# A two-block network on one core: the recurrences of layer 0 taken apart, with GEMMs put between their pieces

## Chip, core and metric

The kernel runs on one core of one Trainium2 chip. The metric is the device time of one execution in microseconds (us); most executions of a kernel agree within 0.3%. The engines are TensorE (PE; its weight loads are PEld), VectorE (DVE), ScalarE (ACT), GpSimd (POOL) and SyncE (SP, which issues most DMAs). They run side by side and wait for one another by semaphores.

## What is computed

The program is a two-layer network for 512 tokens of width 1024, followed by a second network of one layer. Each of the two layers has a mixer and a mixture of 16 experts. Only the mixer of layer 0 is touched. It projects its input once and feeds two branches: a bidirectional gated recurrence over 512 channels with a gate of its own, and a Hyena branch of 512 channels, two long convolutions done by FFT matrices. `_adaln` gives the shifts, scales and gates ("modulation") of both layers from one vector, a product with a 1024 x 6144 matrix per layer.

```python
def _adaln(cvec, w_mod, b_mod, n_chunks):
    m = jax.nn.silu(cvec) @ w_mod[:, :n_chunks * D_MODEL] + b_mod[:n_chunks * D_MODEL]
    return [m[:, None, j * D_MODEL:(j + 1) * D_MODEL] for j in range(n_chunks)]

def _rglru(xa_raw, p, h0):
    xa = _dwconv1d(xa_raw, p['conv_a_w'], p['conv_a_b'])
    ...
    r = gate(p['lru_wr'], p['lru_br'])          # sigmoid of a product per head
    i = gate(p['lru_wi'], p['lru_bi'])
    log_a = -LRU_C * r * jax.nn.softplus(-p['lru_lam'].astype(f32))[:, None, None, :]
    a = jnp.exp(log_a)
    u = jnp.sqrt(-jnp.expm1(2.0 * log_a)) * i * xa.astype(f32)[None]
    ...
    a_cum, h = lax.associative_scan(_lin_combine, (a, u), axis=2)
    ...

def _even_mixer(h, p, h0):
    proj = h @ p['w_in']
    gate = proj[..., :RNN_WIDTH]
    xa_raw = proj[..., RNN_WIDTH:2 * RNN_WIDTH]
    hy = proj[..., 2 * RNN_WIDTH:]
    hs, h_last = _rglru(xa_raw, p, h0)
    y_a = jax.nn.gelu(gate) * (hs[0] + jnp.flip(hs[1], axis=1)).astype(h.dtype)
    u = _dwconv1d(hy, p['conv_b_w'], p['conv_b_b'])
    v, *gates = jnp.split(u, HYENA_ORDER + 1, axis=-1)
    kf = _hyena_filters_fft(h.shape[1], p)
    z = v
    for o in range(HYENA_ORDER):
        z = gates[o] * _fftconv(z, kf[:, o], p['filt_bias'][o])
    return jnp.concatenate([y_a, z], axis=-1) @ p['w_out'], h_last
```

The recurrence's initial state comes from a context of 256 tokens, so a scan runs over 256 and then 512 tokens, in both directions.

## The kernel before, around the change

The activations lie with channels on the partitions: a channel tile `ct` is 128 channels by 512 tokens. Layer 0 (`layer0`) works the Hyena branch in two halves of 256 channels, and the recurrence in two pairs of channel tiles. Its order in the program:

- the filter spectra `K` of the first Hyena half, the first modulation block, the normalization;
- in one scope: `hyena_in(0, "mm")`, the first half's input products; `hyena(.., 0, ..)`, its convolutions, with the modulation unit (0, 1) fed between its steps; the products that enter the recurrence, `xax` and, for the context, `xac`;
- in the next scope: `lru` for channel tiles 0 and 1, then `lru` for 2 and 3, with the modulation units (0, 2) and (1, 0) fed into them; then the second half's `filters`; then its input products, `hyena_in(1, "ac")`;
- in a third scope: `hyena(.., 1, ..)`; then the four GEMMs of the recurrence's gate with GELU, multiplied into `cat`; then `part`, which splits each finished channel tile in a high and a low fp32r half, and `project`, the output projection, which ends in the routing of the experts.

A GEMM (`gemm_block`, `gemm3`, L351) takes 24 matmuls of 128x512 in fp32r: eight steps of the contraction, three products of halves. Its weights come as a block of 1 MB (`cblock`, `rload`, L318), good for two GEMMs; each GEMM's half of it is split by an ACT copy (`wsplit`, L340, tile `wsh`) and a subtraction (`sub`, L334, tile `wsl`), of which every third goes to POOL and the others to DVE. After a GEMM, `conv_tap` evicts it (ACT, L629) and adds the other taps on DVE (L635).

`lru` has two parts: for each channel tile, matmuls (L653) and tanh (L655) of the gates, tanh and exp (L660, L661) and a DVE product (L663); then for both tiles one square root (L668), two DVE products (L670, L671), eight scans (L674, L675) and a POOL sum (L677). Its tiles `lr` and `li` have two buffers, one for each channel tile of a pair; `lt`, of both tiles, has one.

`filters` first makes ten sums and differences in the tile `filtF` (matmuls L593, DVE L594 to L616, some on POOL), then 18 matmuls (L623) for `K`.

A modulation unit (l, i) is eight blocks of 1 MB; `mod_mm` (L448) issues four matmuls a block, the profile records each fp32 matmul twice. `mod_units` is a generator: `mod_feed(n)` runs n blocks of it. The blocks have the tile `mblk` with two buffers.

What sets the order. Each engine and each DMA queue executes its instructions in a fixed order, made when the program is built: a scheduler takes the instructions in program order, but lets a later one that is ready go ahead while an earlier one waits. A tile is given out by a pool: `ring` has four buffers of 1 MB for all streamed weights; PSUM has eight banks under three tags, `mm` (four), `tr` (two) and `ac` (two). A pool that is opened after another was closed may lie on its memory, and its tiles then wait for the earlier ones to be done with. `project` writes its end (`TAIL`) in an order by hand, and the experts' loads (`expert_load`) follow on SP's queue, behind four reloads of `x` (L811) into the memory that `z` and `xac` had.

Of the kernel before, what the change touches and what calls it, by code (L numbers as in the profile page):

```python
# [10 lines left out]
F32 = mybir.dt.float32  # L11
# [7 lines left out]
P = 128  # L19
# [250 lines left out]
class Builder:  # L270
# [214 lines left out]
    def mod_units(self, mp, tag, units, bufs):  # L485

        nc, a = self.nc, self.a
        for l, i in units:
            p = self.mm(tag)
            for k in range(KD):  # L490
                w = mp.tile([P, 2048], F32, tag="mblk", name=self.nm("mblk"), bufs=bufs)
                nc.sync.dma_start(out=w, in_=a["w_mod"][l, k * P:(k + 1) * P, 2048 * i:2048 * (i + 1)])
                self.mod_mm(p, w, k)
                if k < KD - 1:
                    yield
            if i:

                r = slice(0, 64) if i == 1 else slice(64, 128)
                nc.vector.tensor_tensor(self.modr[r, l], p[r], self.modr[r, l], op=ALU.add)
            q = self.mod_turn(mp, p)  # L500
            for h, n, b in {0: ((0, 0, "bsh1"), (1, 1, "bsc1")), 1: ((1, 2, "bsh2"),), 2: ((0, 3, "bsc2"),)}[i]:
                self.mod_put(self.modc[:, l, n], q, h, 0, self.col(b, 8 * l, 8))
            yield
# [134 lines left out]
    def lru(self, kp, wp, cts, xac, xax, hb, s2, s4, cat):  # L638

        nc, a = self.nc, self.a  # L640
        st = []
        tt = wp.tile([P, 2, 2, 768], F32, tag="lt", name=self.nm("lt"))
        for ct in cts:
            lw = kp.tile([P, 512], F32, tag="gt", name=self.nm("lruw")).rearrange("p (g c) -> p g c", g=4) if ct % 2 else \
                wp.tile([P, 4, P], F32, tag="lruw", name=self.nm("lruw"))
            nc.gpsimd.dma_start(out=lw, in_=a["lruw"][:, ct * 512:(ct + 1) * 512].rearrange("p (g c) -> p g c", g=4))
            r, i = (wp.tile([P, 2, 768], F32, tag=n, name=self.nm(n), bufs=2) for n in ("lr", "li"))
            t = tt[:, len(st)]
            for xa, o, n in ((xac[:, ct], 0, 256), (xax[:, ct], 256, 512)):
                for d in range(2):  # L650
                    for g, dst in ((0, r), (1, i)):
                        p = self.mm()
                        nc.tensor.matmul(p[:, :n], lw[:, 2 * d + g], xa, start=True, stop=True)  # L653

                        nc.scalar.activation(out=dst[:, d, o:o + n], in_=p[:, :n], func=AF.Tanh, scale=0.5,  # L655
                                             bias=hb[:, 8 * g + 4 * d + ct:8 * g + 4 * d + ct + 1])

            for d in range(2):
                c = slice(4 * d + ct, 4 * d + ct + 1)
                nc.scalar.activation(out=t[:, d], in_=r[:, d], func=AF.Tanh, scale=s2[:, c], bias=s2[:, c])  # L660
                nc.scalar.activation(out=r[:, d], in_=r[:, d], func=AF.Exp, scale=s4[:, c], bias=s4[:, c])  # L661
            for xa, o, n in ((xac[:, ct], 0, 256), (xax[:, ct], 256, 512)):
                nc.vector.scalar_tensor_tensor(i[:, :, o:o + n], i[:, :, o:o + n], 1.0, xa[:, None, :].to_broadcast([P, 2, n]),  # L663
                                               op0=ALU.add, op1=ALU.mult)
            st.append((ct, r, i, t))
            self.mod_feed(4)
        f = lambda x: x.rearrange("p d n -> p (d n)")
        nc.scalar.activation(out=tt, in_=tt, func=AF.Sqrt)  # L668
        for ct, r, i, t in st:
            nc.vector.scalar_tensor_tensor(f(t), f(r), 1.0, f(t), op0=ALU.add, op1=ALU.mult)  # L670
            nc.vector.scalar_tensor_tensor(f(t), f(t), 0.5, f(i), op0=ALU.mult, op1=ALU.mult)  # L671
            for o, n, ini in ((0, 256, (0.0, 0.0)), (256, 512, (i[:, 0, 255:256], i[:, 1, 0:1]))):
                s = slice(o, o + n)
                nc.vector.tensor_tensor_scan(i[:, 0, s], r[:, 0, s], t[:, 0, s], ini[0], op0=ALU.mult, op1=ALU.add)  # L674
                nc.vector.tensor_tensor_scan(i[:, 1, s][:, ::-1], r[:, 1, s][:, ::-1], t[:, 1, s][:, ::-1], ini[1],  # L675
                                             op0=ALU.mult, op1=ALU.add)
            nc.gpsimd.tensor_tensor(cat[:, ct], i[:, 0, 256:768], i[:, 1, 256:768], op=ALU.add)  # L677

    def layer0(self):
        nc, a, tc = self.nc, self.a, self.tc  # L680
        es = ExitStack()
        kp = es.enter_context(tc.tile_pool(name="A", bufs=1, reuse_waits="tile"))
        cat = kp.tile([P, KD, 512], F32, name="cat0")
        self.fc0 = kp.tile([P, 2, P], F32, name="fc0")
        K = kp.tile([P, 9, 2, 256], F32, name="K")
        self.h2 = kp.tile([65, 512], F32, name="h2")
        self.nrow0 = kp.tile([P, 3], F32, name="nrow0")
        lam = kp.tile([P, 2, 8], F32, name="lamc")
        hb = kp.tile([P, 16], F32, name="lruhb")
        x = self.x  # L690
        w = ExitStack()
        wp = w.enter_context(tc.tile_pool(name="A1", bufs=1, reuse_waits="tile"))
# [8 lines left out]
        rt, fcs = self.filter_blocks(0, fpool)  # L701

        wn = ExitStack()
        wq = wn.enter_context(tc.tile_pool(name="A2n", bufs=1, reuse_waits="tile"))
# [39 lines left out]
        z = xf[:, 0:3072].rearrange("p (q c n) -> p q c n", q=3, c=2)  # L744
        xac = xf[:, 3072:4096].rearrange("p (c n) -> p c n", c=4)
        xax = cat[:, 0:4]

        def hyena_in(hf, tag):
            for q in range(3):
                wt = self.cblock(wi, (1024 + 512 * q + 256 * hf, 256))  # L750
                for c in range(2):
                    ct = 4 * q + 2 * hf + c
                    p = self.gemm_block(kp, wt, c, h, tag)
                    self.conv_tap(z[:, q, c], p, 512, "cbw", self.col("cbb", ct), ct, 12, 1, 3)
                yield


        w = ExitStack()
        wp = w.enter_context(tc.tile_pool(name="A4", bufs=1, reuse_waits="tile"))
# [18 lines left out]

        w = ExitStack()
        wp = w.enter_context(tc.tile_pool(name="A2", bufs=1, reuse_waits="tile"))  # L780
        mw = ExitStack()
        self.mod_begin(mw.enter_context(tc.tile_pool(name="Amb", bufs=1, reuse_waits="tile")), "tr", ((0, 2), (1, 0)))
        self.lru(kp, wp, (0, 1), xac, xax, hb, lam[:, 0], lam[:, 1], cat)
        self.lru(kp, wp, (2, 3), xac, xax, hb, lam[:, 0], lam[:, 1], cat)
        self.mod_end()
        mw.close()
        wq = w.enter_context(tc.tile_pool(name="A3", bufs=1, reuse_waits="tile"))
        rt, fcs = self.filter_blocks(1)
        list(self.filters(wq, rt, fcs, K, "ac"))
        for _ in hyena_in(1, "ac"):  # L790
            pass
        w.close()

        w = ExitStack()
        wp = w.enter_context(tc.tile_pool(name="A4b", bufs=1, reuse_waits="tile"))
        self.hyena(wp, 1, K, z)
        for q in range(2):
            wt = self.cblock(wi, (256 * q, 256))
            for c in range(2):
                ct = 2 * q + c  # L800
                p = self.gemm_block(kp, wt, c, h, "ac")
                gt = kp.tile([P, 512], F32, tag="gt", name=self.nm("gt"))
                last = nc.scalar.activation(out=gt, in_=p, func=AF.Gelu_apprx_tanh)
                nc.gpsimd.tensor_tensor(cat[:, ct], cat[:, ct], gt, op=ALU.mult)
        parts = self.hparts("cp")
        for ct in range(6):
            self.part(parts, ct, cat[:, ct])
# [7 lines left out]
        w = ExitStack()  # L815
        wp = w.enter_context(tc.tile_pool(name="A5", bufs=1, side="right", reuse_waits="tile"))
        gate = self.bcast_gate(wp, 0, 0)
# [1654 lines left out]
```

## Time and profile before

| | |
|---|---|
| time, median of 3 runs | 2370.78 us (2370.53 to 2378.63) |
| the profiled execution's own time | 2370.2 us |
| its span, first to last instruction | 2368.1 us |
| mean granted clock of TensorE | 0.963 |
| busy share of the span: PE, DVE, ACT, POOL | 92%, 43%, 26%, 15% |
| read from HBM, mean rate | 545.51 MB, 232 GB/s |

A busy time is the union of an engine's instructions. The matmuls' ends are modelled, so that a busy TensorE is not one at its peak; the granted clock is given as a share of full speed. The layers' mixtures of experts and the second network take most of the span; the stage of the change is some 185 us long.

### The profile page before, as it was taken

How to read it: one execution, taken by the hardware profiler on the slowest of the kernel's cores; microseconds unless marked ns; L12 is line 12 of the kernel's file. 1: busy time of each engine (PE TensorE's matmuls, PEld its weight loads, DVE VectorE, ACT ScalarE, POOL GpSimd, SP SyncE). 2: the span in 40 equal slices, each digit the busy share in tenths (PEclk: the TensorE clock that was granted, in tenths of full speed). 3: DMA queues.
4: the chain of work that ended last, by engine and by line, in shares of the span. 5: the costliest groups of instructions: out<-in, count | busy, mean ns of one | idle time of the engine just before them, and what ended most of it. 6: DMA issues, size and time to landing. Idle time of an engine off the chain costs nothing.

```text
span 2368.1 us, 29818 instructions
## 1 busy us (share of the span) xinstructions
PE 2183.7 (92%) x11928; PEld 1319.5 (56%) x11928; DVE 1025.3 (43%) x2051; ACT 614.8 (26%) x1149; POOL 361.0 (15%) x390
## 2 busy tenths in 40 slices
PE   7997899999998987999899998987999889999998
PEld 2772487554342424667554433334766667777776
DVE  5645563622121214883522221215665666535642
ACT  3336123210000004333200000005433334333442
POOL 2221113000000002012000000002233431232232
PEclk9998799989999999999889999998999999999999
DMA  8537215679999997744789999996211220141131
GB/s 323 190 106 266 107 61 209 244 321 419 418 419 418 419 419 274 249 160 160 301 324 420 420 420 420 420 418 207 71 37 46 79 63 28 37 151 45 45 112 71
DMA packets 190196, 551.64 MB, mean 233 GB/s; under 512 B 12625, under 2 KB 69849, under 8 KB 182762
## 3 DMA queue, kind: packets, MB, share of 16 engines
q1 hardware_dynamic: 186282, 533.47, 58.4%
q0 software_dynamic: 2768, 11.71, 1.5%
q10 hardware_dynamic: 1008, 4.56, 0.5%
q8 instruction: 94, 1.54, 0.3%
q14 instruction: 44, 0.36, 0.0%
HBM read 545.51 MB, written 4.19 MB: 232 GB/s over the span
## 4 chain that ended last, share of the span: by engine, by line
PE 60%; DMA 13%; DVE 5%; POOL 3%; ACT 2%; issue 1%; POOLq 0%; DVEq 0%; ACTq 0%; SPq 0%
PE mm L1166 14%; DMA ring<-in_exp_w_dram 12%; PE ac L1166 6%; PE ac L1553 4%; PE mm L904 4%; PE ac L1554 4%; PE ac L1555 4%; PE mm L351 4%; PE mm L1662 2%; PE tr L1127 2%; PE ac L351 2%; PE ac L1127 2%; PE ac L1275 1%; PE tr L1275 1%; PE tr L1710 1%
## 5 line engine op out<-in xcount | busy, mean ns | idle before, releaser
L1166 PE MATMUL mm<-ring,xsT 128*64 128x512 f32 x2048 | 472.2, 596 | 38.1 <-DMA ring<-in_exp_w_dram 38.1
L1166 PEld LDWEIGHTS mm<-ring,xsT 128*64 128x64 f32 x2048 | 149.8, 137 | 328.1 <-issue 250.0
L1166 PE MATMUL ac<-ring,em 128*64 128x512 f32 x896 | 203.9, 601 | 13.2 <-DMA ring<-in_exp_w_dram 12.3
L1553 PE MATMUL ac<-hC,sth 128*128 128x512 f32 x504 | 211.5, 420 | 1.7 <-ACT msg L2249 1.7
L1554 PE MATMUL ac<-hC,sth 128*128 128x512 f32 x504 | 206.5, 410 | 0.0
L1555 PE MATMUL ac<-hC,stl 128*128 128x512 f32 x504 | 204.4, 406 | 0.2 <-DVE stl L334 0.2
L1166 PEld LDWEIGHTS ac<-ring,em 128*64 128x64 f32 x896 | 64.7, 138 | 142.1 <-issue 111.3
L1529 ACT ACTIVATE sth<-ring 128x512 fp32r<-128x512 f32 x126 | 79.2, 630 | 145.9 <-PE ac L1554 127.7
L1255 DVE TENSOR_TENSOR em<-em,mm 128x512 f32<-128x512 f32 x32 | 21.8, 688 | 218.9 <-PE mm L1166 216.9
L1553 PEld LDWEIGHTS ac<-hC,sth 128*128 128x128 f32 x504 | 96.6, 192 | 25.9 <-ACT msg L2249 4.0
L1267 DVE SCALAR_TENSOR_TENSOR ac<-ac,gts,gate 128x512 f32<-128x512 f32 x28 | 21.2, 759 | 204.5 <-PE ac L1166 204.5
L1555 PEld LDWEIGHTS ac<-hC,stl 128*128 128x128 f32 x504 | 96.2, 191 | 20.9 <-DVE stl L334 0.7
L1554 PEld LDWEIGHTS ac<-hC,sth 128*128 128x128 f32 x504 | 96.4, 191 | 20.1 <-issue 2.1
L1276 DVE TENSOR_TENSOR x<-ac,x 128x512 f32<-128x512 f32 x64 | 41.6, 686 | 140.8 <-PE ac L1275 140.8
L334 POOL TENSOR_TENSOR wsl<-ring,wsh 128x1024 fp32r<-128x1024 f32 x7 | 16.7, 2386 | 547.8 <-ACT wsh L340 547.8
L904 PE MATMUL mm<-pwh,cp 128*128 128x512 f32 x256 | 86.2, 416 | 4.6 <-ACT cp L1473 3.2
L334 DVE TENSOR_TENSOR stl<-ring,sth 128x512 fp32r<-128x512 f32 x84 | 63.1, 752 | 62.6 <-ACT sth L1529 60.7
L351 PE MATMUL mm<-hB,wsh 128*128 128x512 f32 x256 | 85.1, 407 | 1.5 <-ACT hB L418 0.7
L1254 ACT ACTIVATE em<-mm 128x512 f32<-128x512 f32 x32 | 18.9, 597 | 238.6 <-PE mm L1166 238.6
L334 POOL TENSOR_TENSOR stl<-ring,sth 128x512 fp32r<-128x512 f32 x42 | 54.4, 1295 | 154.7 <-ACT sth L1529 154.4
L1268 ACT ACTIVATE ey<-ac 128x512 fp32r<-128x512 f32 x28 | 16.7, 597 | 212.0 <-PE ac L1166 209.4
L351 PE MATMUL ac<-hA,wsh 128*128 128x512 f32 x224 | 71.4, 399 | 0.0
(804 smaller groups left out, 3840.4 us busy)
## 6 DMA issues: line engine op xcount, KB each, us to landing
ring<-in_exp_w_dram SPq DMA_DIRECT2D x384, 1024.0 KB, 17.8
ring<-in_w_in_dram SPq DMA_DIRECT2D x40, 1024.0 KB, 5.2
mblk<-in_w_mod_dram SPq DMA_DIRECT2D x40, 1024.0 KB, 5.0
ring<-in_cf_w_dram SPq DMA_DIRECT2D x12, 1024.0 KB, 8.0
ring<-in_w_out_dram SPq DMA_DIRECT2D x8, 1024.0 KB, 5.1
ring<-in_w_mod_dram SPq DMA_DIRECT2D x4, 1024.0 KB, 21.9
hW<-in_w_mod_dram SPq DMA_DIRECT2D x4, 1024.0 KB, 23.6
wbr<-in_w_branch_dram SPq DMA_DIRECT2D x16, 256.0 KB, 2.6
```

Of the source, the lines that this page charges most:

```text
L334: (self.nc.gpsimd if self.nlo % self.lomod == 0 else self.nc.vector).tensor_tensor(out, a, b, op=ALU.subtract)
L351: self.nc.tensor.matmul(p[:, :n], x[:, k], y[:, k], start=(k == 0 and i == 0), stop=(stop and k == K - 1 and i == 2))
L904: nc.tensor.matmul(ps[t], u, v[:, k], start=(bias is None and s == 0 and k == 0 and i == 0), stop=(s == 3 and k == 1 and i == 2))
L1127: nc.tensor.matmul(pk, xn[i][:, t, k * P:(k + 1) * P], oh[:, t, 0:len(qs)].rearrange("p q s -> p (q s)"), start=(i == t == 0), stop=(i == ...
L1166: nc.tensor.matmul(ps[j][64 * s:64 * s + 64, :], lhs(k, s), wt[s][:, kk, j * 512:(j + 1) * 512], start=(k == 0), stop=(k == KD - 1))
L1275: nc.tensor.matmul(p, sc[:, t * P:(t + 1) * P], e[:, i], start=(i == 0), stop=(i == 1))
L1276: nc.vector.tensor_tensor(x[:, t, js], p, x[:, t, js], op=ALU.add)
L1529: nc.scalar.activation(out=hi, in_=src, func=AF.Copy)
L1553: nc.tensor.matmul(self.sps, hi[:, k], hh, start=(kk == 0), stop=False)
L1554: nc.tensor.matmul(self.sps, hi[:, k], hl, start=False, stop=False)
L1555: nc.tensor.matmul(self.sps, lo[:, k], hh, start=False, stop=(kk == KD - 1))
L1662: self.nc.tensor.matmul(p[s], lb[:, c], r, start=start, stop=stop)
```

## The change

`mod_units` can take its blocks from the ring (`bufs` 0) and not from two buffers of its own. `lru` becomes a generator that stops between the gates of its pair and the square root and scans, and feeds two modulation blocks per channel tile, not four. In `layer0` the two recurrences and the second half's three pairs of input products (`rows`) are then stepped through in turn: gates of the first pair; two pairs of input products; scans of the first pair; gates of the second pair; the third pair of input products; the first two GEMMs of the gate (`gate(0)`); scans of the second pair; the last two (`gate(1)`). The input products use the PSUM tag `mm` and no longer `ac`. The filters follow. Of the two modulation units that ran within the recurrences, (0, 2) stays there and (1, 0) goes into the second half's Hyena, both through the ring. The first part of the layer is as it was.

```diff
         for l, i in units:
             p = self.mm(tag)
             for k in range(KD):
-                w = mp.tile([P, 2048], F32, tag="mblk", name=self.nm("mblk"), bufs=bufs)
-                nc.sync.dma_start(out=w, in_=a["w_mod"][l, k * P:(k + 1) * P, 2048 * i:2048 * (i + 1)])
+                v = a["w_mod"][l, k * P:(k + 1) * P, 2048 * i:2048 * (i + 1)]
+                if bufs:
+                    w = mp.tile([P, 2048], F32, tag="mblk", name=self.nm("mblk"), bufs=bufs)
+                    nc.sync.dma_start(out=w, in_=v)
+                else:
+                    w = self.rload([(lambda t: t, v)])
                 self.mod_mm(p, w, k)
...
             st.append((ct, r, i, t))
-            self.mod_feed(4)
+            self.mod_feed(2)
+        yield
         f = lambda x: x.rearrange("p d n -> p (d n)")
         nc.scalar.activation(out=tt, in_=tt, func=AF.Sqrt)
...
         w = ExitStack()
         wp = w.enter_context(tc.tile_pool(name="A2", bufs=1, reuse_waits="tile"))
-        mw = ExitStack()
-        self.mod_begin(mw.enter_context(tc.tile_pool(name="Amb", bufs=1, reuse_waits="tile")), "tr", ((0, 2), (1, 0)))
-        self.lru(kp, wp, (0, 1), xac, xax, hb, lam[:, 0], lam[:, 1], cat)
-        self.lru(kp, wp, (2, 3), xac, xax, hb, lam[:, 0], lam[:, 1], cat)
-        self.mod_end()
-        mw.close()
-        wq = w.enter_context(tc.tile_pool(name="A3", bufs=1, reuse_waits="tile"))
-        rt, fcs = self.filter_blocks(1)
-        list(self.filters(wq, rt, fcs, K, "ac"))
-        for _ in hyena_in(1, "ac"):
-            pass
-        w.close()
-
-        w = ExitStack()
-        wp = w.enter_context(tc.tile_pool(name="A4b", bufs=1, reuse_waits="tile"))
-        self.hyena(wp, 1, K, z)
-        for q in range(2):
+        self.mod_begin(w.enter_context(tc.tile_pool(name="Amb", bufs=1, reuse_waits="tile")), "tr", ((0, 2),), 0)
+        rows = hyena_in(1, "mm")
+        rec = [self.lru(kp, wp, c, xac, xax, hb, lam[:, 0], lam[:, 1], cat) for c in ((0, 1), (2, 3))]
+
+        def gate(q):
             wt = self.cblock(wi, (256 * q, 256))
             for c in range(2):
                 ct = 2 * q + c
                 p = self.gemm_block(kp, wt, c, h, "ac")
                 gt = kp.tile([P, 512], F32, tag="gt", name=self.nm("gt"))
                 last = nc.scalar.activation(out=gt, in_=p, func=AF.Gelu_apprx_tanh)
                 nc.gpsimd.tensor_tensor(cat[:, ct], cat[:, ct], gt, op=ALU.mult)
+            return last
+
+
+        next(rec[0])
+        next(rows)
+        next(rows)
+        next(rec[0], None)
+        next(rec[1])
+        next(rows)
+        gate(0)
+        next(rec[1], None)
+        self.mod_end()
+        last = gate(1)
+        wq = w.enter_context(tc.tile_pool(name="A3", bufs=1, reuse_waits="tile"))
+        rt, fcs = self.filter_blocks(1)
+        list(self.filters(wq, rt, fcs, K, "ac"))
+        w.close()
+
+        w = ExitStack()
+        wp = w.enter_context(tc.tile_pool(name="A4b", bufs=1, reuse_waits="tile"))
+        self.mod_begin(w.enter_context(tc.tile_pool(name="Amc", bufs=1, reuse_waits="tile")), "ac", ((1, 0),), 0)
+        self.hyena(wp, 1, K, z)
+        self.mod_end()
         parts = self.hparts("cp")
```

## Rows read from the trace of the kernel before

**Rows 1.** The page: an engine's busy time; the chain that ended last, by line.

```profile
PE 2183.7 (92%) x11928; PEld 1319.5 (56%) x11928; DVE 1025.3 (43%) x2051; ACT 614.8 (26%) x1149; POOL 361.0 (15%) x390
...
PE mm L1166 14%; DMA ring<-in_exp_w_dram 12%; PE ac L1166 6%; PE ac L1553 4%; PE mm L904 4%; PE ac L1554 4%; PE ac L1555 4%; PE mm L351 4%; PE mm L1662 2%; PE tr L1127 2%; PE ac L351 2%; PE ac L1127 2%; PE ac L1275 1%; PE tr L1275 1%; PE tr L1710 1%
```

**Rows 2.** Busy time by stretch: PE, PEld, DVE, ACT, POOL, clock, DMA share, GB/s.

```profile
182.00:248.00 66.00, 44.04 (x189) 13.79 (x188) 41.29 (x40) 35.68 (x46) 7.77 (x7) 0.77 0.73 255
248.00:280.00 32.00, 28.29 (x50) 11.35 (x51) 14.28 (x22) 4.92 (x9) 7.56 (x7) 0.73 0.28 104
280.00:313.00 33.00, 33.00 (x151) 27.38 (x149) 13.74 (x20) 9.78 (x12) 2.40 (x1) 1.00 0.27 93
...
182.00:366.85 184.85, 159.18 (x641) 97.38 (x641) 102.60 (x157) 62.42 (x86) 27.46 (x21) 0.87 0.41 143
```

**Rows 3.** Timeline of ScalarE: start, us, operation, [idle before it, its releaser].

```profile
207.80 1.28 ACT L655 ACT_TABLE_LOAD   x1 [10.41 <-DVE li L675]
209.09 0.47 ACT L655 ACTIVATE lr<-mm,lruhb 128x256 f32<-128x256 f32 x1
```

**Rows 4.** Timeline of VectorE: scans, filters, first and last Hyena product.

```profile
204.71 0.67 DVE L675 TENSOR_TENSOR_SCAN li<-lr,lt 128x256 f32<-128x256 f32 x1
...
208.22 1.69 DVE L675 TENSOR_TENSOR_SCAN li<-lr,lt 128x256 f32<-128x256 f32 x1
...
247.70 1.26 DVE L594 TENSOR_TENSOR filtF<-ac,ring 128x512 f32<-128x512 f32 x2
...
316.25 0.42 DVE L850 TENSOR_TENSOR t<-mm,K 128x256 f32<-128x256 f32 x1 [0.65 <-PE mm L847]
...
351.73 0.69 DVE L870 TENSOR_TENSOR x<-y,x 128x512 f32<-128x512 f32 x1
```

**Rows 5.** Groups by line, 182 to 248 us: busy, mean ns, idle before.

```profile
L448 PE MATMUL tr<-mblk,silc 128*32 128x512 f32 x128 | 22.7, 796 | 16.8 <-DMA mblk<-in_w_mod_dram 16.8
L653 PE MATMUL mm<-cat,lruw 128*128 128x512 f32 x25 | 13.1, 650 | 0.0
```

**Rows 6.** Timeline of TensorE, neighbouring instructions of a line merged.

```profile
185.91 3.60 PE L653 MATMUL mm<-cat,lruw 128*128 128x512 f32 x8
...
217.26 1.07 PE L448 MATMUL tr<-mblk,silc 128*32 128x512 f32 x8
...
248.41 10.61 PE L593 MATMUL ac<-ring,h 65*128 65x512 f32 x12 [4.57 <-DVE filtF L594]
...
366.85 0.50 PE L904 MATMUL mm<-pwh,cp 128*128 128x512 f32 x1
```

**Rows 7.** Groups by line, 248 to 367 us.

```profile
L862 PE MATMUL mm<-ics,Y 128*128 128x256 f32 x64 | 14.5, 379 | 0.0
L847 PE MATMUL mm<-pt,dcs 128*128 128x256 f32 x64 | 14.3, 381 | 0.0
...
L635 DVE SCALAR_TENSOR_TENSOR x<-ac,cols,x 128x511 f32<-128x511 f32 x12 | 9.0, 747 | 2.9 <-ACT x L629 2.6
L340 ACT ACTIVATE wsh<-ring 128x1024 fp32r<-128x1024 f32 x8 | 8.5, 1060 | 26.4 <-PE ac L351 22.5 <-issue 3.8
L334 DVE TENSOR_TENSOR wsl<-ring,wsh 128x1024 fp32r<-128x1024 f32 x6 | 7.3, 1224 | 15.9 <-ACT wsh L340 15.9
...
L334 POOL TENSOR_TENSOR wsl<-ring,wsh 128x1024 fp32r<-128x1024 f32 x2 | 4.8, 2388 | 43.3 <-ACT wsh L340 43.3
...
L629 ACT ACTIVATE x<-ac,cols 128x512 f32<-128x512 f32 x6 | 4.6, 760 | 0.0
```

**Rows 8.** DMA issues, 150 to 400 us: count, KB each, median us to landing.

```profile
ring<-in_w_out_dram SPq DMA_DIRECT2D x4, 1024.0 KB, 5.0
```

**Rows 9.** Timeline of SP's queue: the first expert weights.

```profile
373.71 2.33 SPq L318 DMA_DIRECT2D ring<-in_exp_w_dram  x4
```

**Rows 10.** Waits of SP's queue, 150 to 400 us: total, times, longest.

```profile
SPq L811 <- DVE cp L334: 17.4, 1, 17.4
```

**Rows 11.** Timeline of GpSimd: the sum of the first recurrence.

```profile
207.86 1.50 POOL L677 TENSOR_TENSOR cat<-li 128x512 f32<-128x512 f32 x1 [17.51 <-issue]
```

## The prediction

> **What bounds the kernel now.** I read the page first, then the busy time by stage, then each engine's timeline over the one stage that the diff touches. The page says that TensorE is busy 92% of the span, which seems to leave little; and its chain of waits, summed over the whole span, has no line that only this stage runs (L653, L448, L623) among its fifteen largest [rows 1]. So the chain doesn't price this change, and I take the stage itself: from 182 us, when the last input products of the first half are done, to the first matmul of the output projection at 366.85 us [rows 6]. Over these 184.85 us TensorE is busy 159.18 us at a mean granted clock of 0.87; the reader is to see that the loss lies ahead of 280 us: the clock is 0.77 and then 0.73 there, between its levels of 1.2 and 2.4 GHz, and from 280 us on it is 1.00 and TensorE never idles [rows 2]. A TensorE that is busy at the lower clock does half the work.
>
> Why it is lost there is in the timelines. The recurrences are one serial chain: gates on ScalarE, one square root, multiplies and scans on VectorE. The second pair of channels begins only when the first pair's scans give back the buffers `lr` and `li`: ScalarE waits 10.41 us for `DVE li L675` [rows 3]. The last scan ends at 247.7 us, where L594 follows at once [rows 4]. Beside this chain TensorE has little but the modulation's blocks, and waits 16.8 us for their loads [rows 5]. The filters then hold the rest up: the L593 group of 248.41 us waits for L594 [rows 6], which waited itself, for its tile `filtF` lies in the pool that is opened after the modulation's is closed; the second half's input products want the same two `ac` banks as the filters and come behind them.
>
> **The change, part by part.** *TensorE's work is the floor.* At the full clock, from 182 us to the projection:
> - recurrences: 25 records of 512 columns [rows 5] and as many of 256; eight of 512 take 3.60 us, 0.45 each [rows 6]: 11.3 + 5.6 = 17 us;
> - 16 modulation blocks, 1.07 us each [rows 6]: 17 us;
> - ten GEMMs, six of the input and four of the gate; six fill 280 to 313 us, 33 us [rows 2]: 55 us;
> - filters: 8 + 18 products of two records of 512 columns, 52 x 0.45: 23 us;
> - the second half's Hyena: 14.3 + 14.5 [rows 7]: 29 us.
>
> That is 141 us of 184.85. Transposes, router and gate rows are left out, so 44 us is the most that a full TensorE at full clock gives back.
>
> *Input and gate products between the recurrences.* TensorE's work beside the recurrences becomes 17 + 8 + 55 = 80 us (half the modulation blocks move out), which ends at 262 us at the earliest. The chain of the recurrences was 66 us, and the new products load its engines too. VectorE: 12 taps of 0.747 us and, of ten subtractions, seven of 1.224 us [rows 7] (every third goes to GpSimd): 17.5 us; its 41.29 us become 59 of 66 [rows 2]. ScalarE: ten splits of 1.060 us, and ten evictions of about 0.760 us [rows 7]: 18 us; its 35.68 us become 54 [rows 2]. And GELU among tanh and square root adds table loads of 1.28 us [rows 3]; I count four, 5 us. Both engines still have room, but the new work stands ahead of the scans in program order. Bounds of what it adds to the chain: 0, all of it in the chain's own waits, and 35 us, none of it. I take the middle, 18 us, since the chain has waits as long as 10.41 us [rows 3], but VectorE alone is busy for 41.29 of its 66 us: 182 + 66 + 18 = 266 us.
>
> The rows have ScalarE back at work 0.01 us behind a table load of 1.28 us, at 209.09 us [rows 3]. The Trainium skill (ScalarE: Activation LUTs, section "Table sets: the hidden batching unit") counts about 2.7 us for a switch, and asks for all calls of one set before the next, which this change gives up. By the page four switches would be an estimated 11 us and not 5, and the sum below 6 us higher, 2345; the trace shows no such drain.
>
> *Filters.* `filtF` no longer lies over the modulation's blocks, so L594 can go first wherever VectorE is free. Today the filters' stretch is 32 us with 14.28 us of VectorE [rows 2]; its last part, 36 records of 0.45 us, is 16 us of TensorE. If VectorE's part fits beside the second recurrence, 16 us are left after the scans; if nothing fits, 32. I take 25, nearer to the upper end, because VectorE has only 7 us free of the 66: 291 us.
>
> *Second Hyena half.* From its first product on VectorE (316.25 us) to its last (352.4 us) it is 36 us [rows 4]. The gate GEMMs that fill TensorE's waits there leave; the moved modulation unit brings eight blocks of 1.07 us in their place, so I add nothing: 327 us. Parts of `z` for the projection: 2 us, 329. What of the gate GEMMs runs today between the Hyena's end and the projection, 352 to 366.85 us, is gone from the path. Were the eight blocks not covered, they would cost 9 us.
>
> *Modulation in the ring.* Sixteen blocks now share four buffers with three input blocks, two gate blocks, two of the filters, and on SP's queue they stand ahead of the projection's four. A landing takes 5.0 us [rows 8], less than a GEMM of 5.5 us, so a block that is asked for one GEMM ahead costs nothing: the lower bound. Upper bound: as today's two buffers with nothing else ready, 16.8 us over 16 blocks, 1.05 each [rows 5], over the 13 blocks between the recurrences, 14 us. I take 4 us, nearer to the lower end, because GEMMs are ready. Another 2 us for the wait on `lr` and `li`.
>
> 329 + 6 = 335 us, above TensorE's own sum (182 + 141 = 323): the projection begins 32 us earlier. What follows moves along: the first expert weights are issued at 373.71 us [rows 9], behind the last reload of `x` (L811), for which SP waited 17.4 us on `DVE cp` [rows 10], the parts. So the stream of weights, 12% of the chain [rows 1], starts earlier by the same.
>
> **Sum.** The profiled execution took 2370.2 us (2.1 outside its span of 2368.1), 0.6 under the median 2370.8. 2370.8 - 32 = **2339 us**.
>
> **Rivals.**
> 1. *The recurrences become the path.* A scan of 256 columns takes 0.67 us alone and 1.69 us at 208.22 [rows 4], while GpSimd adds from 207.86 us for 1.50 us [rows 11]. The new work puts on GpSimd three subtractions of 2.388 us [rows 7] and four products of about 1.50 us, 13 us. If that and VectorE's 17.5 us all lengthen the chain, the last scan ends at 182 + 66 + 31 = 279 us; filters 32, Hyena 36, parts 2: 349, a gain of 18: **2353**. Against it: VectorE idles 25 of the 66 us [rows 2]. The Trainium skill (SBUF — State Buffer, section "Summary: rules for kernel authors") states the collision as a rule: of a VectorE operation with two SBUF inputs and a GpSimd operation that reads SBUF, the second waits until the first is done. The trace agrees, by 1.02 us on that scan.
> 2. *No change.* The products stay behind the scans in the engines' order, or the expert stream gains nothing: **2371**. For it: the weights' 12% of the chain. Against it: the first weights hang on the parts, and the input products have nothing to wait for once their banks are `mm`.
> 3. *Slower: the ring starves TensorE.* If each of the 13 blocks between the recurrences shows its whole landing, 13 x 5.0 = 65 us: 2339 + 65 = **2404**. It decides from 32 / 13 = 2.5 us a block. For it: each block's buffer comes free only by a matmul of an earlier one, and TensorE's order is fixed. Against it: today's 1.05 us a block with half the buffers.
> 4. *Better.* The chain's waits take all of the new work and TensorE's sum is the end: a gain of 44, **2327**.
>
> **How the numbers follow.** Forecast (2330 to 2347) 0.60; rival 1 (2347 to 2359) 0.17; rival 2 0.08; rival 3 0.07; rival 4 0.08. Bounds of the unknown costs: the chain longer by all 35 us and the filters at 32 us give a gain of 8, 2363; all at their lower ends meet TensorE's sum, 2327. The range is 2326 to 2358; it leaves out rivals 2 and 3 and the edge of rival 1. Half a per cent, 12 us, is about what a measurement can tell from no change: faster 0.60 + 0.08 + 0.16 = 0.84; same 0.08 + 0.01 = 0.09; slower 0.07.
>
> **What would show it.** A granted clock near 1.0 from 182 us on, where it was 0.77 and 0.73. L351 matmuls into `mm` between gates and scans; L448's wait for loads under 5 us in sum. The first L594 before the last scan. The last scan near 266 us, the last L870 near 327, the first L904 near 335, the first expert load near 342. The forecast is wrong if the last scan ends after 280 us (rival 1), if waits for the ring's blocks pass 20 us (rival 3), or if the experts do not start earlier by what the projection does (rival 2).

## The result, and the profile after

The changed kernel takes **2362.8 us** (median of 11 runs, 2356.8 to 2368.4) against 2375.1 us of the kernel before in runs on the same chips: ratio 0.9945, 95% interval 0.9932 to 0.9958, some 13 us faster by the ratio (12.3 by the medians) where 32 were forecast (2339, range 2326 to 2358): little more than the half per cent that the prediction took to be just measurable, and outside the range. From L593 on the changed file's lines lie 4 further down, from L663 on 4 or 5, and Hyena and projection 16 (L862 is L878, L904 is L920).

Busy time by stretch, changed kernel (columns and stretches as in [rows 2], two more, and up to the projection):

```profile
182.00:248.00 66.00, 57.54 (x228) 34.46 (x227) 37.17 (x38) 45.70 (x57) 8.40 (x6) 0.91 0.54 178
248.00:280.00 32.00, 27.93 (x112) 22.51 (x111) 26.18 (x23) 8.19 (x10) 11.29 (x7) 0.91 0.29 108
280.00:313.00 33.00, 29.27 (x98) 17.20 (x98) 18.31 (x26) 7.65 (x14) 11.41 (x8) 1.00 0.21 75
182.00:356.12 174.12, 156.99 (x645) 100.09 (x643) 110.91 (x159) 71.38 (x98) 32.37 (x22) 0.95 0.46 159
...
272.00:286.00 14.00, 13.13 (x49) 10.15 (x49) 5.88 (x6) 1.29 (x3) 5.61 (x6) 0.88 0.62 225
286.00:309.00 23.00, 19.27 (x65) 11.03 (x65) 17.69 (x25) 5.17 (x10) 10.12 (x7) 1.00 0.14 47
```

The clock did what was forecast: 0.91, 0.91 and 1.00 where it was 0.77, 0.73 and 1.00 [rows 2]. The stage still takes 174.12 us, not 153. TensorE's timeline, then SyncE's first expert load:

```profile
272.87 0.50 PE L351 MATMUL ac<-hA,wsl 128*128 128x512 f32 x1 [4.07 <-DVE wsl L334]
...
284.81 0.40 PE L351 MATMUL ac<-hA,wsl 128*128 128x512 f32 x1
285.05 2.93 PE L597 MATMUL ac<-ring,h 65*128 65x512 f32 x6
...
356.12 0.73 PE L920 MATMUL mm<-pwh,cp 128*128 128x512 f32 x2
```

```profile
360.62 1.60 SPq L318 DMA_DIRECT2D ring<-in_exp_w_dram  x3
```

The projection begins 10.7 us earlier than in [rows 6], the expert weights 13.1 us earlier than in [rows 9]. The first expert matmul is at 431.6 us instead of 444.6, and the lead is still 13.0 us at the second layer's projection (1049.2 instead of 1062.2). So the gain, and what it lacks of the forecast, arise inside the stage. The two profiled executions end only 2.3 us apart (spans of 2368.1 and 2365.8 us), since behind that projection, in code that the change does not touch, the changed kernel's has lower granted clocks, as 0.91 against 1.00 in the 100 us from some 2100 us on. VectorE's timeline shows where:

```profile
260.33 2.23 DVE L679 TENSOR_TENSOR_SCAN li<-lr,lt 128x256 f32<-128x256 f32 x1
...
263.12 0.68 DVE L680 TENSOR_TENSOR_SCAN li<-lr,lt 128x256 f32<-128x256 f32 x1
...
268.29 2.23 DVE L679 TENSOR_TENSOR_SCAN li<-lr,li,lt 128x512 f32<-128x512 f32 x1
270.44 1.25 DVE L680 TENSOR_TENSOR_SCAN li<-lr,li,lt 128x512 f32<-128x512 f32 x1
271.62 1.19 DVE L334 TENSOR_TENSOR wsl<-ring,wsh 128x1024 fp32r<-128x1024 f32 x1
...
286.11 0.69 DVE L598 TENSOR_TENSOR filtF<-ac,ring 128x512 f32<-128x512 f32 x1 [8.22 <-PE ac L597]
...
308.60 0.69 DVE L620 TENSOR_TENSOR filtF<-filtF 128x512 f32<-128x512 f32 x1 [1.37 <-POOL filtF L619]
```

The last scan ends at 271.7 us, the first filter sum comes at 286.11 and had waited 8.22 us for its product, the last sum ends at 309.3, the last copy into `K` at 321.3. In the kernel before the first sum stood directly behind the last scan [rows 4]. The 14.4 us between them are new, and in them TensorE does gate(1)'s 48 matmuls, which themselves waited 4.07 us for a subtraction behind the last scan.

### The profile page after: what moved, and what is told of

Read it like the earlier page. It is cut to its first block, busy times and chain, and to the rows that moved or that the text cites. A ratio compares the mean times of both kernels' runs of the same rounds, so it can differ in the third digit from the quotient of the medians.

```text
span 2365.8 us, 29806 instructions
## 1 busy us (share of the span) xinstructions
PE 2189.7 (93%) x11928; PEld 1328.3 (56%) x11928; DVE 1028.7 (43%) x2049; ACT 616.4 (26%) x1151; POOL 362.8 (15%) x390
## 4 chain that ended last, share of the span: by engine, by line
PE 60%; DMA 13%; DVE 5%; POOL 3%; ACT 1%; issue 1%; SPq 0%; POOLq 0%; DVEq 0%; ACTq 0%
PE mm L1182 13%; DMA ring<-in_exp_w_dram 12%; PE ac L1182 6%; PE ac L1569 4%; PE mm L920 4%; PE ac L1570 4%; PE ac L1571 4%; PE mm L351 4%; PE mm L1678 2%; PE tr L1143 2%; PE ac L351 2%; PE ac L1143 2%; PE ac L1291 1%; PE tr L1291 1%; PE tr L1726 1%
## 5 line engine op out<-in xcount | busy, mean ns | idle before, releaser
L1182 PE MATMUL ac<-ring,em 128*64 128x512 f32 x896 | 205.1, 604 | 13.1 <-DMA ring<-in_exp_w_dram 12.2
L1283 DVE SCALAR_TENSOR_TENSOR ac<-ac,gts,gate 128x512 f32<-128x512 f32 x28 | 21.2, 758 | 205.6 <-PE ac L1182 205.6
L920 PE MATMUL mm<-pwh,cp 128*128 128x512 f32 x256 | 85.0, 411 | 3.8 <-ACT cp L1489 3.2
L351 PE MATMUL mm<-hB,wsh 128*128 128x512 f32 x256 | 85.2, 408 | 1.3 <-ACT hB L418 0.7
```

What stands on the lines that cost most here:

```text
L351: self.nc.tensor.matmul(p[:, :n], x[:, k], y[:, k], start=(k == 0 and i == 0), stop=(stop and k == K - 1 and i == 2))
L920: nc.tensor.matmul(ps[t], u, v[:, k], start=(bias is None and s == 0 and k == 0 and i == 0), stop=(s == 3 and k == 1 and i == 2))
L1182: nc.tensor.matmul(ps[j][64 * s:64 * s + 64, :], lhs(k, s), wt[s][:, kk, j * 512:(j + 1) * 512], start=(k == 0), stop=(k == KD - 1))
```

## The experiments

Each change is against the changed kernel unless another is named. Marks are read from each trace, one execution of each kernel, in us; ratios are to the kernel before, run beside it.

| | last scan | `K` done | Hyena's last matmul | first expert matmul | median | ratio, interval |
|---|---|---|---|---|---|---|
| before | 247.8 | 280.4 | 349.6 | 444.6 | 2375.1 | 1 |
| after | 271.7 | 321.3 | 355.1 | 431.6 | 2362.8 | 0.9945 (0.9932 to 0.9958) |
| e1 | 270.7 | 318.6 | 355.7 | 430.4 | 2359.7 | 0.9925 (0.9907 to 0.9943) |
| e2 | 271.6 | 325.3 | 361.4 | 436.5 | 2369.0 | 0.9961 (0.9942 to 0.998) |
| e3 | 272.4 | 322.7 | 358.1 | 434.3 | 2367.6 | 0.9956 (0.9939 to 0.9972) |
| e4 | 251.7 | 272.9 | 348.0 | 449.9 | 2379.3 | 1.0019 (1.0003 to 1.0035) |
| e5 | 271.5 | 320.9 | 355.9 | 429.9 | 2362.1 | 0.9938 (0.9919 to 0.9956) |
| e6 | 272.0 | 320.2 | 354.3 | 430.5 | 2362.2 | 0.9936 (0.9918 to 0.9954) |
| e7 | 284.1 | 308.3 | 362.9 | 438.8 | 2373.6 | 0.9984 (0.9972 to 0.9996) |
| e8 | 268.0 | 310.3 | 349.0 | 422.4 | 2354.0 | 0.9902 (0.9884 to 0.9919) |
| e9 | 270.8 | 310.7 | 356.2 | 434.2 | 2364.6 | 0.9943 (0.9923 to 0.9963) |
| e10 | 270.1 | 316.0 | 351.5 | 427.8 | 2357.8 | 0.9912 (0.9895 to 0.9929) |
| e11 | 265.8 | 308.5 | 345.9 | 419.6 | 2356.6 | 0.9920 (0.9905 to 0.9935) |
| e12 | 265.9 | 308.7 | 346.3 | 420.1 | 2358.6 | 0.9934 (0.992 to 0.9949) |

**e1: the filters' banks.**

```diff
-        list(self.filters(wq, rt, fcs, K, "ac"))
+        list(self.filters(wq, rt, fcs, K, "mm"))
```

> Only the PSUM tag of the second half's filters changes, from ac to mm; TensorE's order stays. Theory A (order: the filters' products stand behind gate(1)'s 48 matmuls on TensorE, which is full from 244 to 285 because it was starved from 219 to 241): first filter product still at about 285, first expert matmul at 431.6 within 4 us, 2361 to 2365 us. Theory B (banks: the products wait for ac banks that gate(1)'s blocks hold until their gelu and the sums give them back): the first filter sum comes right behind its product, the 8.2 us of wait ahead of it is gone, K is done some 8 us earlier, first expert matmul at 424 or earlier, about 2353 to 2356 us.

The first sum still waits behind gate(1) for its product:

```profile
284.84 0.69 DVE L598 TENSOR_TENSOR filtF<-mm,ring 128x512 f32<-128x512 f32 x1 [8.01 <-PE mm L597]
```

First expert matmul 1.2 us earlier: theory A, and the banks are not what holds the first sum.

**e2: gate(1) behind the filters' products.**

```diff
-        last = gate(1)
...
-        list(self.filters(wq, rt, fcs, K, "ac"))
+        spectra = self.filters(wq, rt, fcs, K, "ac")
+        next(spectra)
+        last = gate(1)
+        list(spectra)
```

> gate(1)'s two blocks are put behind the filters' eight first products and sums, ahead of their transforms; no work is added or removed. Theory A (order): first filter product at about 270, sums directly behind the last scan (271.7 to 295), gate(1)'s 12 us of TensorE under the sums, last K copy at about 307 instead of 321, first expert matmul 10 to 14 us earlier than 431.6, about 2350 us. Theory C (the way behind the filters is bound elsewhere: VectorE with scans, sums and the Hyena products, or the modulation's loads): K is earlier, but the first expert matmul by less than 4 us, 2359 to 2363 us.

`K` comes 4 us later and the first expert matmul 4.9 us later: neither theory's numbers. The windows of this run, and two lines of TensorE, say why:

```profile
272.00:282.00 10.00, 6.70 (x14) 3.42 (x15) 9.20 (x11) 1.17 (x2) 4.14 (x4) 0.59 0.67 243
282.00:292.00 10.00, 10.00 (x18) 5.52 (x17) 4.69 (x7) 0.00 (x0) 2.82 (x2) 0.50 0.17 72
292.00:302.00 10.00, 10.00 (x40) 7.64 (x39) 6.19 (x9) 0.00 (x0) 2.72 (x3) 0.88 0.31 105
```

```profile
274.22 0.66 PE L858 MATMUL tr<-ident,fold 128*128 128x128 f32 x2 [5.14 <-DVE fold L853]
...
297.64 0.82 PE L351 MATMUL ac<-hA,wsh 128*128 128x512 f32 x2
```

Behind the first of the eight products stand transposes of `fold`, the sums and differences with which Hyena begins; VectorE makes them behind the last scan, and TensorE waits for them for 5.14 and, once more, 1.08 us, its only waits from 268 to 300 us. Its granted clock falls to 0.50, the 1.2 GHz level, and gate(1), in order behind the other products and Hyena's first 28 records (L865), starts only at 297.6 us, when the sums are nearly done: it lies in front of the transforms and not beneath the sums.

**e3: the third input row ahead of the second gates.**

```diff
-        next(rec[1])
         next(rows)
+        next(rec[1])
```

> The third input row (its weights' splits on ScalarE, 48 matmuls, four taps) is put ahead of the second unit's gates; the rest stays. Theory A (TensorE starved from 219 to 241 while ScalarE alone worked): the 48 matmuls fill that hole, gate(1) ends some 10 us earlier (275 instead of 285), first expert matmul 8 to 11 us earlier, about 2353 us. Theory D (ScalarE and VectorE are the chain there): the splits and the block's first taps put the gates and so the second scans back by 4 to 6 us, last scan at 275 or later, sums no earlier, first expert matmul within 3 us of 431.6 or later, 2361 to 2366 us.

```profile
219.00:241.00 22.00, 20.88 (x91) 12.51 (x89) 11.51 (x14) 11.20 (x17) 2.18 (x1) 1.00 0.38 122
262.00:272.00 10.00, 3.09 (x13) 1.92 (x11) 10.00 (x9) 1.54 (x2) 4.32 (x3) 0.84 0.00 0
```

From 219 to 241 us TensorE is now busy 20.88 us instead of 17.47; the last scan ends at 272.4 as in the changed kernel, and TensorE has its hole from 262 to 272 us instead, where VectorE is busy throughout. First expert matmul 2.7 us later: theory D by this mark, though the last scan is only 0.7 us later and not at 275. The scans' chain sets this part, and to fill TensorE's hole from 219 to 241 us gains nothing.

**e4: the modulation's part alone.** Recurrences whole, input products behind the filters, gate products behind Hyena as in the kernel before; units (0, 2) and (1, 0) as in the changed one.

```diff
-        next(rec[0])
...
-        last = gate(1)
+        for r in rec:
+            for _ in r:
+                pass
+        self.mod_end()
...
+        for _ in hyena_in(1, "ac"):
+            pass
...
         self.hyena(wp, 1, K, z)
+        for q in range(2):
+            last = gate(q)
         self.mod_end()
```

> The modulation's part of the change alone: unit (0,2) in the recurrences and unit (1,0) in the second half's Hyena, both with blocks in the ring; recurrences not split, input products behind the filters, gate products behind Hyena as before. If the gain of 13 us came from the split and the interleaving: first expert matmul within 4 us of before's 444.6, 2371 to 2376 us. If the modulation's move alone carries it (the recurrences lose eight blocks and their load waits, 17 us of wait before): first expert matmul at 431 to 436, 2360 to 2366 us. My estimate lies between: 438, some 2368 us.

Slower than every expectation. VectorE, with the first sum of the filters at the top, and ScalarE:

```profile
212.67 0.69 DVE L598 TENSOR_TENSOR filtF<-ac,ring 128x512 f32<-128x512 f32 x1
...
250.42 1.25 DVE L680 TENSOR_TENSOR_SCAN li<-lr,li,lt 128x512 f32<-128x512 f32 x1
251.59 0.66 DVE L605 TENSOR_TENSOR filtF<-filtF 128x512 f32<-128x512 f32 x1
...
257.27 0.69 DVE L620 TENSOR_TENSOR filtF<-filtF 128x512 f32<-128x512 f32 x1 [1.38 <-POOL filtF L619]
```

```profile
354.29 0.60 ACT L796 ACTIVATE gt<-ac 128x512 f32<-128x512 f32 x1
...
368.77 0.58 ACT L796 ACTIVATE gt<-ac 128x512 f32<-128x512 f32 x1
```

Here the forecast's step on `filtF` came true: all but three of VectorE's sums stand ahead of the last scan, and `K` is done 21.2 us behind it, inside the forecast's 16 to 32. But Hyena, which now has the modulation in it, gives nearly 6 of the 7.4 us back (its last matmul is 1.6 us earlier), and the four GELUs of the gate, of which the first stood at 335 us within Hyena before, all come behind it.

**e5: the interleaving alone**, with the modulation as in the kernel before.

```diff
-            self.mod_feed(2)
+            self.mod_feed(4)
...
-        self.mod_begin(w.enter_context(tc.tile_pool(name="Amb", bufs=1, reuse_waits="tile")), "tr", ((0, 2),), 0)
+        mw = ExitStack()
+        self.mod_begin(mw.enter_context(tc.tile_pool(name="Amb", bufs=1, reuse_waits="tile")), "tr", ((0, 2), (1, 0)))
...
         self.mod_end()
+        mw.close()
         last = gate(1)
...
-        self.mod_begin(w.enter_context(tc.tile_pool(name="Amc", bufs=1, reuse_waits="tile")), "ac", ((1, 0),), 0)
         self.hyena(wp, 1, K, z)
-        self.mod_end()
```

> The other part alone: recurrences split, input and gate products between them as in the changed kernel, but the modulation as before (both units, sixteen blocks, all in the recurrences with two buffers of their own). Modulation alone gave +4 us, first expert matmul 449.9 against 444.6. If the interleaving carries the gain and the modulation's move adds nothing: first expert matmul 430 to 434, 2360 to 2364 us. If the two belong together (sixteen blocks with their load waits lengthen the recurrences): first expert matmul 436 to 442, 2367 to 2371 us. I take the second.

The first guess holds, to 0.1 us, and the one that I took does not: the interleaving carries all of the gain. Sixteen blocks with two buffers hurt little now, with other products beside them: TensorE waits 2.5 us for their loads from 182 to 360 us, where it waited 16.8 us [rows 5]. And Hyena has a gap again:

```profile
322.00:332.00 10.00, 7.61 (x34) 6.18 (x34) 8.36 (x21) 2.25 (x4) 0.00 (x0) 1.00 0.00 0
332.00:342.00 10.00, 8.86 (x17) 4.29 (x18) 2.38 (x5) 1.78 (x3) 0.00 (x0) 0.54 0.16 52
```

It is a gap in useful work more than an idle stretch: from 329.7 to 338.9 us TensorE is busy for 6.24 us at a granted clock of 0.67, with little but transposes.

**e6: gate(1)'s weights split ahead of the second scans** (`wsplit` for both of its GEMMs ahead of `next(rec[1], None)`).

> gate(1)'s weights are loaded and split before the second scans instead of behind them; TensorE's order stays. TensorE's idle 4.07 us behind VectorE's subtraction (271.6) is gone. Theory A (TensorE's queue ahead of the filters): gate(1) ends 3 to 5 us earlier, at about 281, first filter product and first expert matmul as much earlier (427 to 428.5), about 2359 us. Theory D (VectorE is the chain): the subtractions of 1.2 us each stand between scans, last scan 1 to 3 us later, first expert matmul within 2 us of 431.6.

The wait moved from gate(1)'s first GEMM to its second, whose subtraction now stands behind Hyena's folds on VectorE; first expert matmul 1.1 us earlier. That is theory D's number for the experts, but the last scan is only 0.3 us later, and theory A's 3 to 5 us did not come:

```profile
277.27 0.50 PE L351 MATMUL ac<-hA,wsl 128*128 128x512 f32 x1 [3.51 <-DVE wsl L334]
```

**e7: the filters' sums ahead of the second scans.**

```diff
         next(rec[0], None)
-        next(rec[1])
         next(rows)
+        next(rec[1])
+        wq = w.enter_context(tc.tile_pool(name="A3", bufs=1, reuse_waits="tile"))
+        rt, fcs = self.filter_blocks(1)
+        spectra = self.filters(wq, rt, fcs, K, "ac")
+        next(spectra)
         gate(0)
+        list(spectra)
         next(rec[1], None)
         self.mod_end()
         last = gate(1)
-        wq = w.enter_context(tc.tile_pool(name="A3", bufs=1, reuse_waits="tile"))
-        rt, fcs = self.filter_blocks(1)
-        list(self.filters(wq, rt, fcs, K, "ac"))
```

> Third input row ahead of the second gates; the filters' loads, products and sums ahead of the second scans, transforms behind gate(0), gate(1) last. Theory E (the filters' step of 49.5 us behind the last scan is the loss, because VectorE's sums and TensorE's transforms can begin only when scans and gate(1) are done, while VectorE is 30 to 37% busy from 222 to 242): sums under the second gates, K done before 285, Hyena's first products follow at once, first expert matmul 15 to 25 us earlier than 431.6, 2338 to 2348 us. Theory C (what follows is full anyway: TensorE at work 90% of the time from 182 to 355 in the changed kernel, and the second scans come late behind sums): first expert matmul by 0 to 6 us earlier, 2357 to 2363 us.

Worse than both (the edit holds that of e3 too, which cost 2.7 us by itself). The sums do begin early, at 247.79 us, and `K` is 13 us earlier, but scans, sums and splits now alternate in VectorE's queue, and TensorE stands between them at the low clock:

```profile
262.00:272.00 10.00, 3.79 (x9) 3.08 (x10) 9.33 (x12) 0.00 (x0) 0.86 (x2) 0.50 0.23 74
...
282.00:292.00 10.00, 2.56 (x5) 0.98 (x5) 5.68 (x8) 1.55 (x3) 7.75 (x5) 0.73 0.35 113
```

**e8 and e9: gate(1) in Hyena's gap.** e9 is the changed kernel with this edit, e8 is e5 with it.

```diff
-        last = gate(1)
...
-        self.hyena(wp, 1, K, z)
+        last = []
+        self.hyena(wp, 1, K, z, lambda: last.append(gate(1)))
+        last = last[0]
...
         for o in range(2):
+            if o and mid:
+                mid()
```

> Interleaving as in the changed kernel, modulation as before (both units in the recurrences), and gate(1) put between the two orders of the second half's Hyena, where the run of the interleaving alone leaves TensorE idle for some 9 us (329.7 to 338.9). Theory F (of the filters' 49.5 us behind the last scan, 13 are gate(1) in front of them, and they are paid in full because nothing else of the chain runs then): last scan at 271 to 272, K done at 304 to 308 instead of 320.9, first expert matmul at 417 to 421 against 429.9, about 2350 us. Theory G (what gate(1) gives up is lost again: TensorE idles under the sums, its granted clock falls to half, and gate(1) lengthens Hyena): K at 306 to 312, first expert matmul at 427 or later, 2359 to 2363 us.

> The changed kernel with gate(1) between the two orders of Hyena and nothing else. Theory F: K done at 304 to 308 instead of 321.3; in Hyena gate(1) meets the sixteen modulation blocks' matmuls, so less of it is hidden than without them: first expert matmul at 420 to 424 against 431.6, about 2353 us. Theory G: first expert matmul at 430 or later, 2362 us or more.

In e8 the last scan is 3.5 us earlier than in e5, which neither theory had, the first sum is 7.1 us behind it and `K` done at 310.3 us, inside theory G's range and 2 us behind theory F's; the first expert matmul is 7.5 us earlier than in e5, between the two theories and 1.4 us short of theory F. `K` is 10.6 us earlier than in e5, but from there to Hyena's last matmul 38.7 us pass, where it was 35.0. TensorE's clock is low under the first sums:

```profile
272.00:282.00 10.00, 8.66 (x19) 4.71 (x20) 7.97 (x11) 1.77 (x3) 1.93 (x3) 0.58 0.83 305
...
322.00:332.00 10.00, 10.00 (x54) 8.15 (x53) 3.98 (x9) 5.85 (x11) 5.58 (x5) 0.98 0.17 52
332.00:342.00 10.00, 10.00 (x41) 8.52 (x41) 9.67 (x25) 2.51 (x5) 1.18 (x1) 0.85 0.00 0
```

But Hyena's gap of e5 is full (last two lines). e9 has `K` as early as e8, and its first expert matmul is 11.8 us later, theory G's number: modulation (eight blocks here, not sixteen) and gate(1) want the same gap. TensorE is busy from 322 to 352 us almost without a break, at a clock of 1.00, and from `K` to Hyena's last matmul it takes 45.5 us instead of 33.9 in the changed kernel. 2354.0 us is the best of both kernels and all runs here, though e11's interval overlaps.

**e10: no subtraction of the splits on GpSimd** (`self.lomod` out of reach from the first gates to gate(1)).

> The changed kernel with every subtraction of the weight splits between the first gates and gate(1) on VectorE; the changed kernel gives one in three to GpSimd. Theory H (GpSimd's share of the port makes VectorE's scans slow: scans of 2.23 us instead of 1.26 and 0.68, and a GpSimd subtraction of 3.54 us): no subtraction of GpSimd in 182 to 285, scans at 0.68 and 1.25 but for those that meet the sums of cat and the gates' products, last scan 2 to 3 us earlier (269), first expert matmul 1 to 3 us earlier. Rival: the three or four subtractions that VectorE takes over cost it 1.2 us each in the same queue, last scan at 271 to 274, first expert matmul within 2 us of 431.6 or later.

```profile
257.44 0.68 DVE L679 TENSOR_TENSOR_SCAN li<-lr,lt 128x256 f32<-128x256 f32 x1
...
266.65 2.24 DVE L679 TENSOR_TENSOR_SCAN li<-lr,li,lt 128x512 f32<-128x512 f32 x1
```

The scan at 260.33 us that took 2.23 us takes 0.68 here. The second tile's scans, which meet GpSimd's sums and gate products, stay slow (2.24). Last scan 1.6 us earlier, less than theory H said; the first sum 5.3 us earlier (280.83), since a subtraction for gate(1) now stands among the scans (263.28 us) and its first GEMM need not wait for the last of them; first expert matmul 3.8, a little more than theory H said.

**e11 and e12: e8 with e10's edit**, in e11 up to the filters, in e12 up to the projection.

> The two edits that gained, together: interleaving with the old modulation and gate(1) between Hyena's two orders, and VectorE for every subtraction of the splits up to the filters (from the filters on one in three goes to GpSimd again, gate(1) among them). If the two gains are of different stages they add: first expert matmul at 418 to 420 (422.4 less the 3.8 us that the second edit gave alone), about 2350 us. If both shorten the same wait (last scan and the queue behind it): 421 to 423, 2353 to 2355 us.

> As the run beside it, and gate(1)'s and the parts' subtractions stay on VectorE too, up to the projection. If GpSimd's subtractions hold VectorE up in Hyena as well: first expert matmul another 1 to 3 us earlier than beside it. If VectorE, which Hyena's products fill, is what is short there: 1 to 4 us later.

By the first expert matmul the gains add (419.6, 25 us ahead of the kernel before). By the medians e8 and e11 cannot be told apart: their intervals overlap, and single runs of one kernel here lie up to 14 us apart. e12 has the same marks within 0.6 us: neither guess.

## Why the prediction was wrong in size

**Sign and direction were right.** The clock rose to 0.91 and more; L351 products into `mm` stand between gates and scans; no wait for a block of the modulation of as much as 0.5 us shows on TensorE, so the ring's rival is dead; and the expert weights are issued 13.1 us earlier, the projection 10.7.

**The step that failed is the filters' term**, "I take 25: 291 us". It measured 49.6 us (271.7 to 321.3): 14.4 to the first sum, 23.2 of sums, 12.0 to the last copy. I let the sums go "wherever VectorE is free" and bounded the term by 16 and 32 with nothing in front of them. The change puts GEMMs in front. In my sum the ten GEMMs had a place on TensorE only in its floor, never in the chain; yet the filters' sums need products that TensorE makes behind them, and by my own floor TensorE was not free before 262 us. Where nothing stood in front (e4), the sums began at 212.67 us, between the scans, and the step held: 21.2 us.

The miss of 24.6 us against the rows: the 14.4 us ahead of the first sum, in which TensorE does gate(1); 2.5 us by which the sums take longer than in the kernel before (23.2 against 20.7, with four subtractions for the projection's parts among them now); and 7.7 us, from the 32.7 us that the filters take behind the last scan in the kernel before down to my 25, for sums that I let run ahead of the last scan, none of which did. The first part is tested: to take gate(1) out, and nothing else, brings `K` 10.5 us earlier (e9 against the changed kernel) or 10.6 (e8 against e5); counted from the last scan, which comes a little earlier too, the term falls to 40.0 and 42.4. The 7.1 us that stay ahead of the sums in e8 are folds and two subtractions of the splits. The sums themselves are a chain of VectorE and GpSimd with waits of 1.4 us, and TensorE's clock did not shorten it: 20.7 us in the kernel before, at a granted clock of 0.57, 22.4 in e9 at 0.66, 23.3 in e8 at 0.81, 23.2 in the changed kernel at 1.00.

That moving gate(1) alone does not bring the experts forward (e2, and e9 with the modulation in the gap) shows that the loss is of order and place, not of one wait: in e2 gate(1) comes back in front of the transforms, in e9 Hyena gives the 10.5 us back. Hyena has one gap, which the change gave to the modulation. The modulation needed no new place (e5).

The measured 2362.8 us meets my worst case of 2363 by luck: that case had the recurrences' chain longer by 35 us and the filters at 32, and they took 24 and 49.6.

**Smaller terms.** The recurrences' chain ended at 271.7 instead of 266: the inserted work cost 24 us of the bounds 0 and 35, where I took 18. Part of it is rival 1's mechanism: e10 takes out the wide subtraction of GpSimd, and 1.6 us with it. The Trainium skill (SBUF — State Buffer, section "Summary: rules for kernel authors") lets a VectorE operation with two SBUF inputs and a GpSimd read go only one after the other. The trace agrees, and both sides pay: the scan at 260.33 us took 2.23 us for 0.68, while GpSimd subtracted from 258.47 us on for 3.54, and in e10 a GpSimd sum of `cat` 4.33 us, where another took 1.26.

Hyena's last product (L886) came at 358.1 us instead of 327, 36.8 us behind `K`: the term of 36 came out, in part by luck, for it was read from Hyena's first product on VectorE, which now runs at 309.21 us, ahead of `K`'s end. The projection begins before it, with the tiles of `cat`; of the 8 us that I added for parts and waits nothing shows on the path. So 5.7, 24.6 and 0.8 us too late, less those 8 and the 2 by which it begins before that product, make the 21.1 us by which the projection missed 335.

**The table loads** cost what their row said, each. ScalarE, changed kernel:

```profile
240.64 2.00 ACT L340 ACTIVATE wsh<-ring 128x1024 fp32r<-128x1024 f32 x2
242.65 1.28 ACT L673 ACT_TABLE_LOAD   x1
...
263.85 1.28 ACT L796 ACT_TABLE_LOAD   x1
265.14 0.60 ACT L796 ACTIVATE gt<-ac 128x512 f32<-128x512 f32 x1
```

Four from 182 to 330 us, work 0.01 to 0.02 us behind each. The kernel before has three there, so the change adds one, 1.28 us, and not the four (5 us) of my count. The 2.7 us of the Trainium skill (ScalarE: Activation LUTs, "Table sets: the hidden batching unit") do not show. The first line is the price of program order instead: the third row's splits had stood behind 20 us of gates.

What stays open is how much of the scans' delay is order (taps and splits between the scans) and how much the shared port; only the subtractions were taken away.

## What to carry to other kernels

When GEMMs are moved into a serial stage, ask of each what stands directly behind it in every engine's order, and enter it in the chain as well as in the busy sum. Look for the gaps of each stretch first, and give each to the work that is now in somebody's way: here the modulation had a free place and took the only gap that gate(1) could use. A chain of small operations on VectorE and GpSimd, like the sums here, need not get shorter with a higher clock of TensorE.

## What the hardware showed that was not expected

A hole in TensorE's work cost more than its own length. In e2 12 us of matmuls were taken from ahead of the sums; TensorE waited there for 5.14 and 1.08 us, was busy 6.70 of the 10 us from 272 us on at a granted clock of 0.59, and then the whole of 10 us at 0.50. From 276.66 to 297.64 us, 21.0 us, it did seven products of the filters and 28 records of Hyena; in the changed kernel, with gate(1) in front and the clock under the sums at 1.00, eight products and 30 records took 17.1 us (285.05 to 302.15). Where VectorE's sums were the chain, the clock did not decide: in e9 it was 0.66 under them, and they took 22.4 us, where they took 23.2 in the changed kernel at 1.00.
